# Gate and up products of the three FFNs as seven block products

## The chip, the core and the metric

The kernel runs on one core of a Trainium2 chip. Its time is the device time of one execution in microseconds (us), from the first to the last instruction. Every number of the kernel before comes from its three timed executions or from one execution that the hardware profiler recorded.

## What is computed

The reference is two transformer blocks in float32 on one sequence of 512 tokens with 1024 features. Each block has a mixer (two kinds of attention in the first, sparse attention and retention in the second); between and behind them lie three gated feed-forward networks (FFN), here called f0, f1 and f2, with 2816 hidden features:

```python
def swiglu(xn, w_gate, w_up, w_down):
    return (jax.nn.silu(xn @ w_gate) * (xn @ w_up)) @ w_down
...
h = rms_norm(x, g);  x = x + 1.0 * swiglu(h, ...)     # f0
h = _rmsnorm(x, g);  x = x + 0.5 * _swiglu(h, ...)    # f1 and f2
```

The two products `xn @ w_gate` and `xn @ w_up` (512 x 1024 by 1024 x 2816 each) are what the change touches.

## The kernel before

Features lie on the partitions: `xh[m]`, `xl[m]` (m = 0..7) are [128, 512] tiles that hold the normalised input (for the FFNs: gain times x, still without its rms) in two exact parts, high and low, and a weight tile is split in the same way. Every product is three matmuls, high x high, high x low and low x high (`mm3`, lines 241 to 245).

`Stream` (lines 141 to 189) brings in the weights in the order of their use, which `plan` (lines 330 to 415) lists. For each item SP issues one DMA into a `raw` tile (line 160, three buffers), ScalarE rounds it to the high part `wh` (line 172), VectorE subtracts for the low part `wl` (line 174, two halves), both in four buffers. `run_ahead` keeps the split two items ahead of the use.

`ffn` (lines 1022 to 1069) goes over two halves of 11 column blocks of 128 hidden features. For one block the gate and the up weights (128 columns, all 1024 rows, 512 KB each, 512-byte rows) are two items; each meets the eight input tiles in 8 x 3 matmuls of 512 columns, so a block is 48 matmuls. Then VectorE multiplies both sums by the rms (`rb`, lines 1042 and 1044), ScalarE takes a tanh (1043), GpSimd multiplies (1045), VectorE multiplies (1046), and the hidden block is split into `hh`, `hl` (1047 to 1052). After 11 blocks the down product runs over eight output tiles with 33 matmuls each (1056 to 1069); in f2's second half `last` (line 1636) does that with tokens on partitions. There are 3 x 22 = 66 such blocks.

In f1 the hook `each` (line 1593) also multiplies one residual tile in blocks 1 to 8. In f2 `out2` (line 1624) transposes the residual while the first half's down product runs. `rb` of an FFN is ready only in its second block (hooks `sums`, `spread`).

The order of instructions on each engine is made at build time by a list scheduler from the program's order and its dependences; every engine then works through its queue in order. The GpSimd queue (POOL) issues few DMAs: the residual's loads in `out_product` (line 1011) and some in the mixers.

Of the kernel before, what the change touches and what calls it, by code (L numbers as in the profile page):

```python
# [49 lines left out]
# columns of the constants  # L50
# [15 lines left out]
# the packed vectors, in pieces of 128  # L66
# [60 lines left out]

def _arrays(inputs):
    """The inputs as the chip takes them: x with features first, the small vectors side by side."""
# [6 lines left out]
    out["pos"] = np.ascontiguousarray(raw["positions"].reshape(NT, P).T)  # L136
    out["cst"], out["ret"], out["rot"] = _constants()
# [3 lines left out]
class Stream:  # L141
    """Weights in the order of their use: loads run ahead, and the split into two exact parts too."""

    def __init__(self, b, plan, raw_bufs, bufs, ahead):
        self.b, self.plan = b, plan
        self.raw_bufs, self.bufs, self.ahead = raw_bufs, bufs, ahead
        self.loaded = self.split = self.used = 0
        self.raw, self.parts = {}, {}

    def load_to(self, n):  # L150
        while self.loaded < min(n, len(self.plan)):
            i = self.loaded
            key, nk, nc_, srcs = self.plan[i]
            t = self.b.wpool.tile([P, 1024], F32, tag="raw", name=f"raw{i}", bufs=self.raw_bufs)
            v = t[:, :nk * nc_].rearrange("p (k n) -> p k n", k=nk)
            for (k0, k1, c0, c1, src) in srcs:
                dst = v[:, k0:k1, c0:c1]
                if key in ("qn", "qr", "kv"):
                    dst = v[:, k0, c0:c1].rearrange("p (h d) -> p h d", h=8)
                self.b.nc.sync.dma_start(out=dst, in_=src)  # L160
            self.raw[i] = (t, nk * nc_)
            self.loaded += 1

    def split_to(self, n):
        nc = self.b.nc
        while self.split < min(n, len(self.plan)):
            i = self.split
            self.load_to(i + 1)
            t, n_el = self.raw.pop(i)
            h = self.b.wpool.tile([P, 1024], F32R, tag="wh", name=f"wh{i}", bufs=self.bufs)  # L170
            lo = self.b.wpool.tile([P, 1024], F32R, tag="wl", name=f"wl{i}", bufs=self.bufs)
# [5 lines left out]
            self.load_to(self.split + self.raw_bufs)  # L177

    def next(self, key):
        i = self.used  # L180
        got, nk, nc_, _ = self.plan[i]
# [3 lines left out]
        h, lo = self.parts.pop(i)  # L185
        return tuple(a[:, :nk * nc_].rearrange("p (k n) -> p k n", k=nk) for a in (h, lo))

    def run_ahead(self):
        self.split_to(self.used + self.ahead)


class Build:
# [28 lines left out]
    def weave(self, main, fill, main_ns, fill_ns, k=1.0):  # L221
        """Interleave two generators of pieces by their share of TensorE's time."""
# [25 lines left out]
    def tgroup(self, acc, pairs, per=1):  # L248
        """pairs: (weight hi, weight lo, x hi, x lo) for each contraction tile"""
# [1461 lines left out]
```

## Time and profile before

| | |
|---|---|
| timed executions | 2122.47, 2123.30, 2123.37 us; median 2123.3 us |
| profiled execution | span 2124.0 us from first to last instruction, 0.7 us above that median |
| TensorE (PE) busy | 2084.2 us, 98% |
| VectorE (DVE) busy | 1359.0 us, 64% |
| ScalarE (ACT) busy | 895.5 us, 42% |
| GpSimd (POOL) busy | 395.1 us, 19% |
| mean transfer rate | 105 GB/s |

PE's busy time counts overlapping matmuls once; a matmul's own duration is longer than the distance to the next, so its pace is read from the starts of neighbours in the timeline. "PEclk" is the granted TensorE clock as a share of 2.4 GHz, "DMA share" the mean busy share of the 16 DMA engines.

### The profile page before, as it was taken

The numbers are of one execution on the slowest core, as the hardware profiler recorded it, in microseconds if no ns is written. First come the engines' busy times: TensorE is split into PE (matmuls) and PEld (weight loads), VectorE is DVE, ScalarE is ACT, GpSimd is POOL, SyncE is SP. The second block draws the span as 40 slices with busy tenths as digits, with TensorE's granted clock in tenths as the row PEclk, the third lists the DMA queues.
The fourth block names the chain that finished last, engine by engine and source line by source line (L and its number), as shares of the span: only waits on it lengthen the run. The fifth ranks groups of instructions, "written<-read, shape, count | busy, mean of one in ns | idle before, by whom it ended". The sixth has DMA issues, their size and how long they took to land.

```text
span 2124.0 us, 27104 instructions
## 1 busy us (share of the span) xinstructions
PE 2084.2 (98%) x9858; PEld 1716.7 (81%) x9858; DVE 1359.0 (64%) x2675; ACT 895.5 (42%) x1637; POOL 395.1 (19%) x360
## 2 busy tenths in 40 slices
PE   8999999999999999999998999999999999999998
PEld 7787878888888888888887778888888888888887
DVE  7778876654455565445547799888557765544655
ACT  5666753322222433223234476666343332323334
POOL 3233332110011220000115121110312221000110
PEclk9999999999999999999999999999999999999999
DMA  5323354332332333233245413222533443323344
GB/s 151 98 62 89 93 170 129 91 91 82 115 91 80 110 98 93 82 113 100 80 143 154 105 55 90 70 80 70 180 114 108 135 149 89 87 83 110 97 118 150
DMA packets 347782, 223.35 MB, mean 105 GB/s; under 512 B 16784, under 2 KB 326160, under 8 KB 347648
## 3 DMA queue, kind: packets, MB, share of 16 engines
q1 hardware_dynamic: 341264, 203.94, 33.4%
q0 software_dynamic: 5024, 15.90, 2.4%
q10 hardware_dynamic: 1360, 1.77, 0.3%
q8 instruction: 78, 1.28, 0.3%
q14 instruction: 56, 0.46, 0.1%
HBM read 204.11 MB, written 14.68 MB: 103 GB/s over the span
## 4 chain that ended last, share of the span: by engine, by line
PE 90%; DVE 4%; ACT 2%; issue 1%; DMA 1%; POOL 1%; SPq 0%; ACTq 0%; POOLq 0%; DVEq 0%
PE mm L243 25%; PE mm L245 25%; PE mm L244 24%; PE pt L477 2%; PE pv L496 1%; PE pv L497 1%; PE mm L1653 1%; PE s L1424 1%; PE s L1425 1%; PE pt L1653 1%; PE pv L1495 1%; DVE wl L174 1%; DMA raw<-in_w_in 1%; PE pt L538 0%; ACT P L459 0%
## 5 line engine op out<-in xcount | busy, mean ns | idle before, releaser
L243 PE MATMUL mm<-xh,wh 128*128 128x512 f32 x1752 | 704.7, 402 | 6.5 <-ACT kvg L1087 6.5
L174 DVE TENSOR_TENSOR wl<-raw,wh 128x512 fp32r<-128x512 f32 (+5 forms) x738 | 551.5, 777 | 216.6 <-ACT wh L172 215.6
L245 PE MATMUL mm<-xh,wl 128*128 128x512 f32 x1752 | 688.7, 393 | 0.0
L244 PE MATMUL mm<-xl,wh 128*128 128x512 f32 x1752 | 687.7, 393 | 0.0
L172 ACT CAST wh<-raw 128x1024 fp32r<-128x1024 f32 (+5 forms) x369 | 360.6, 977 | 734.7 <-PE mm L244 642.5
L245 PEld LDWEIGHTS mm<-xh,wl 128*128 128x128 f32 x1752 | 329.8, 188 | 73.4
L243 PEld LDWEIGHTS mm<-xh,wh 128*128 128x128 f32 x1752 | 330.8, 189 | 66.9 <-ACT kvg L1087 6.7
L244 PEld LDWEIGHTS mm<-xl,wh 128*128 128x128 f32 x1752 | 330.8, 189 | 59.9 <-DVE xl L217 0.6
L1045 POOL TENSOR_TENSOR fu<-fu,fg 128x512 f32<-128x512 f32 x66 | 88.5, 1341 | 809.5 <-DVE fu L1044 809.5
L1044 DVE TENSOR_TENSOR fu<-mm,rb 128x512 f32<-128x512 f32 x66 | 45.6, 691 | 208.5 <-PE mm L245 208.5
L243 PE MATMUL mm<-hh,wh 128*128 128x512 f32 x440 | 173.0, 393 | 0.0
L244 PE MATMUL mm<-hl,wh 128*128 128x512 f32 x440 | 172.2, 391 | 0.0
L245 PE MATMUL mm<-hh,wl 128*128 128x512 f32 x440 | 171.6, 390 | 0.0
L459 ACT ACTIVATE P<-s,st 128x128 f32<-128x128 f32 (+1 forms) x192 | 101.4, 529 | 63.7 <-DVE st L454 59.4
L212 ACT ACTIVATE hh<-ft 128x512 fp32r<-128x512 f32 x66 | 41.8, 633 | 167.0 <-DVE ft L1046 167.0
L210 ACT CAST ph<-pt 128x128 fp32r<-128x128 f32 x192 | 80.3, 425 | 51.3 <-PE pt L477 50.3
L217 DVE TENSOR_TENSOR pl<-pt,ph 128x128 fp32r<-128x128 f32 x192 | 91.6, 484 | 14.1 <-ACT ph L210 12.6
L454 DVE CUSTOM_DVE_ANT_0 s<-s,cst 128x128 f32<-128x128 f32 (+1 forms) x192 | 93.5, 490 | 8.8 <-PE s L1425 4.6
L245 PEld LDWEIGHTS mm<-hh,wl 128*128 128x128 f32 x440 | 82.6, 188 | 18.8
L243 PEld LDWEIGHTS mm<-hh,wh 128*128 128x128 f32 x440 | 82.7, 188 | 17.8
L244 PEld LDWEIGHTS mm<-hl,wh 128*128 128x128 f32 x440 | 82.7, 188 | 17.4
L477 PE MATMUL pt<-cst,P 128*128 128x128 f32 x480 | 83.4, 274 | 1.2 <-DVE pl L217 0.5
(415 smaller groups left out, 2843.0 us busy)
## 6 DMA issues: line engine op xcount, KB each, us to landing
raw<-in_w_in SPq DMA_DIRECT2D x79, 512.0 KB
raw<-in_ffn_w_gate SPq DMA_DIRECT2D x44, 512.0 KB
raw<-in_ffn_w_up SPq DMA_DIRECT2D x44, 512.0 KB
raw<-in_w_ffn_gate SPq DMA_DIRECT2D x22, 512.0 KB
raw<-in_w_ffn_up SPq DMA_DIRECT2D x22, 512.0 KB
raw<-in_ffn_w_down SPq DMA_DIRECT2D x22, 512.0 KB
raw<-in_ffn_w_down SPq DMA_DIRECT2D x24, 384.0 KB
sp_th<-gt SPq DMA_DIRECT2D x32, 256.0 KB
```

Source lines behind the costliest of these rows:

```text
L172: nc.scalar.copy(h[:, :n_el], t[:, :n_el])
L174: nc.vector.tensor_tensor(out=lo[:, a:e], in0=t[:, a:e], in1=h[:, a:e].bitcast(F32), op=ALU.subtract)
L210: self.nc.scalar.copy(out, in_)
L217: (eng or nc.vector).tensor_tensor(out=out, in0=in_, in1=hi.bitcast(F32), op=ALU.subtract)
L243: mm(acc, lhsT=lh, rhs=rh, start=start, stop=False)
L244: mm(acc, lhsT=lh, rhs=rl, start=False, stop=False)
L245: mm(acc, lhsT=ll, rhs=rh, start=False, stop=stop)
L454: nc.vector.tensor_tensor_reduce(out=b, in0=b, in1=u["mask"][:, 512 - n:512], scale=-u["scale"], scalar=3.0e38, op0=ALU.add, op1=ALU.min, ...
L459: nc.scalar.activation(p, b, AF.Exp, bias=st[:, 0:1], scale=-1.0, accum_out=st[:, 1:2])
L477: nc.tensor.transpose(b[:, j * P:(j + 1) * P], u[f"P{i}"][:, j * P:(j + 1) * P], self.ident)
L1044: nc.vector.tensor_tensor(out=u, in0=acc[1], in1=self.rb, op=ALU.mult)
L1045: nc.gpsimd.tensor_tensor(out=u, in0=u, in1=g, op=ALU.mult)
```

## The change

For 18 of the 22 column blocks of each FFN (all but the first four) the gate and up products together become one unit of seven block products (Winograd's form of Strassen's algorithm). The 2 x 2 matrix of weight blocks has gate and up as one index and the two halves of the 1024 input features as the other; the 2 x 2 matrix of input blocks has the halves of the features and the halves of the 512 tokens. One block product ("quarter") is 4 x 3 = 12 matmuls with 256 columns, so a unit is 84 matmuls.

The host lays out gate and up of a column block side by side, four pieces of [128, 512] a block: u (first and second half of features) and g (the same). From these the stream loads three tiles of 512 KB (X, A, Y) and one of 256 KB (D), in 4 KB and 2 KB rows, and forms the four weight sums in X and Y by four DMAs of 256 KB that add to their destination, issued on the GpSimd queue: two with a piece from memory, two from tile to tile (X on itself, X on Y). D has a buffer ring of its own. Raw buffers go from three to four.

The input sums T1 to T4 (`th`, `tl`, also in two parts) are made by `prepare_t`, one feature pair behind each of the four plain blocks; `prepare_b` then overwrites `xh`, `xl` with the input times the rms, eight tiles, when the four plain blocks are through. In a unit ScalarE copies three intermediate sums out of PSUM, and the D quarter of a unit is put behind the first two quarters of the next (`pending`, `flush`). GpSimd's multiplication per block falls away in units.

Smaller edits: the low part is subtracted in one instruction instead of two halves; f1's residual products go two at a time to blocks 6 to 9; f2's transposes move into `last`; comments are removed.

```diff
-RAW_BUFS, PART_BUFS, AHEAD = 3, 4, 2
+RAW_BUFS, PART_BUFS, AHEAD = 4, 4, 2
+NPLAIN = 4
...
+def _gated(g, u):
+    t = lambda w: w.reshape(2, 4, P, FF // P, P).transpose(3, 2, 0, 1, 4).reshape(FF // P, P, 2, 512)
+    return np.ascontiguousarray(np.concatenate([t(u), t(g)], 2))
...
+    AT = {"X": (512, 1024), "A": (1024, 1024), "Y": (1024, 1024), "D": (512, 512)}
...
+                at, n_el = self.AT[kind]
+                nc.sync.dma_start(out=t[:, :n_el], in_=self.plan[i][2].rearrange("p q n -> p (q n)")[:, at:at + n_el])
...
+    def sum_up(self):
+        add = lambda out, in_: self.b.nc.gpsimd.dma_start(out=out, in_=in_, accum_op=ALU.add)
+        while self.summed < self.loaded:
+            i = self.summed
+            kind = self.plan[i][1]
+            if kind in ("X", "Y"):
+                t = self.raw[i][0]
+                add(t[:, 0:512], self.plan[i][2][:, 0, :])
+                if kind == "X":
+                    self.x = t
+                add(t[:, 512:1024], t[:, 0:512] if kind == "X" else self.x[:, 512:1024])
+            self.summed += 1
...
-            for a, e in ((0, n_el // 2), (n_el // 2, n_el)):
-                nc.vector.tensor_tensor(out=lo[:, a:e], in0=t[:, a:e], in1=h[:, a:e].bitcast(F32), op=ALU.subtract)
+            nc.vector.tensor_tensor(out=lo[:, :n_el], in0=t[:, :n_el], in1=h[:, :n_el].bitcast(F32), op=ALU.subtract)
...
+    def quarter(self, acc, i, at, op, start):
+        wh, wl = self.ws.parts[i]
+        for k in range(4):
+            sl = slice(at + k * P, at + (k + 1) * P)
+            xh, xl = self.operand(op, k)
+            for n, (l, r) in enumerate(((wh, xh), (wh, xl), (wl, xh))):
+                self.nc.tensor.matmul(acc, lhsT=l[:, sl], rhs=r, start=start and k + n == 0, stop=k == 3 and n == 2,
+                                      skip_group_check=True)
+
+    def prepare_t(self, k, gain):
+        nc, V, G = self.nc, self.nc.vector, self.nc.gpsimd
+        y = self.small.tile([P, 2, 512], F32, tag="diag", name=self.nm("y"), bufs=1)
+        for j in range(2):
+            V.scalar_tensor_tensor(out=y[:, j, :], in0=self.xs[k + 4 * j], scalar=gain(k + 4 * j), in1=self.rb, op0=ALU.mult, op1=ALU.mult)
...
+        G.tensor_tensor(out=t[0][:, 0, :], in0=b11, in1=b12, op=ALU.subtract)
+        V.tensor_tensor(out=t[1][:, 0, :], in0=b22, in1=b12, op=ALU.subtract)
+        V.scalar_tensor_tensor(out=t[0][:, 1, :], in0=t[1][:, 0, :], scalar=-1.0, in1=b11, op0=ALU.mult, op1=ALU.subtract)
+        V.scalar_tensor_tensor(out=t[1][:, 1, :], in0=t[0][:, 1, :], scalar=-1.0, in1=b21, op0=ALU.mult, op1=ALU.subtract)
+        for j in range(2):
+            h = self.th[k][:, 2 * j:2 * j + 2, :]
+            self.hi(h, t[j])
+            self.lo(self.tl[k][:, 2 * j:2 * j + 2, :], t[j], h)
+
+    def prepare_b(self, gain):
+        for m in range(KD):
+            if m % 2 == 0:
+                y2 = self.small.tile([P, 2, 512], F32, tag="diag", name=self.nm("y"), bufs=1)
+            n = 256 if m < 4 else 512
+            y = y2[:, m % 2, 0:n]
+            self.nc.vector.scalar_tensor_tensor(out=y, in0=self.xs[m][:, 0:n], scalar=gain(m), in1=self.rb[:, 0:n], op0=ALU.mult, op1=ALU.mult)
+            self.hi(self.xh[m][:, 0:n], y)
+            self.lo(self.xl[m][:, 0:n], y, self.xh[m][:, 0:n])
+
+    def unit(self, key, hh, hl, i):
...
+        self.quarter(r1, A, 0, "B11", True)
+        nc.scalar.copy(e[:, 0:256], r1)
+        self.quarter(r23[:, 256:512], X, 0, "T1", True)
+        nc.scalar.copy(f, r23[:, 256:512])
+        self.flush()
...
+        self.quarter(r1, X, 512, "T2", False)
+        nc.scalar.copy(e[:, 256:512], r1)
...
+        self.quarter(r23[:, 0:256], A, 512, "B21", False)
...
+        self.quarter(r23[:, 256:512], Y, 512, "B22", False)
...
+        V.tensor_tensor(out=g, in0=r23, in1=e, op=ALU.add)
+        nc.scalar.activation(th, g, AF.Tanh, scale=0.5)
...
+        self.quarter(r1, Y, 0, "T3", False)
+        V.scalar_tensor_tensor(out=th, in0=th, scalar=1.0, in1=g, op0=ALU.add, op1=ALU.mult)
+        V.tensor_tensor(out=u2, in0=r1, in1=f, op=ALU.add)
+        V.tensor_tensor(out=th[:, 256:512], in0=th[:, 256:512], in1=u2, op=ALU.mult)
...
+        def rest():
+            self.quarter(r1, DD, 0, "T4", False)
+            V.tensor_tensor(out=th[:, 0:256], in0=th[:, 0:256], in1=r1, op=ALU.mult)
+            self.put_hidden(i, th, -0.5, hh, hl)
+            ws.release(DD)
+        self.pending = rest
...
-    nc = bacc.Bacc("TRN2", target_bir_lowering=False, num_devices=1)
+    nc = bacc.Bacc("TRN2", target_bir_lowering=False, num_devices=1, dynamic_dma_scratch_size=8192)
```

## Rows read from the trace of the kernel before

**Rows 1.** Page, part 1: busy us, share of span, instructions.
```profile
PE 2084.2 (98%) x9858; PEld 1716.7 (81%) x9858; DVE 1359.0 (64%) x2675; ACT 895.5 (42%) x1637; POOL 395.1 (19%) x360
```
**Rows 2.** Page, part 4: the chain that ended last, share by engine.
```profile
PE 90%; DVE 4%; ACT 2%; issue 1%; DMA 1%; POOL 1%; SPq 0%; ACTq 0%; POOLq 0%; DVEq 0%
```
**Rows 3.** Busy time by stretch, one column block of f0 each; last columns clock, DMA.
```profile
421.50:432.50 11.00, 11.00 (x49) 9.02 (x48) 6.41 (x9) 3.29 (x4) 1.30 (x1) 1.00 0.33 95
432.50:443.50 11.00, 11.00 (x49) 9.01 (x48) 6.41 (x9) 3.29 (x4) 1.30 (x1) 1.00 0.34 98
```
**Rows 4.** Timeline of ACT in f0: start, us, instruction, idle before it.
```profile
417.14 1.05 ACT L172 CAST wh<-raw 128x1024 fp32r<-128x1024 f32 x1 [3.85 <-PE mm L244]
...
428.13 1.05 ACT L172 CAST wh<-raw 128x1024 fp32r<-128x1024 f32 x1 [3.85 <-PE mm L244]
```
**Rows 5.** Timeline of PE in the last product: 256 columns between 512.
```profile
2086.76 0.28 PE L1653 MATMUL s<-wh,hh 128*128 128x256 f32 x1
...
2087.46 0.39 PE L1653 MATMUL pt<-wh,hh 128*128 128x512 f32 x1
...
2089.55 0.28 PE L1653 MATMUL s<-wh,hh 128*128 128x256 f32 x1
...
2090.26 0.39 PE L1653 MATMUL pt<-wh,hh 128*128 128x512 f32 x1
```
**Rows 6.** Groups by line and shape: count, busy us, mean ns, idle before.
```profile
L172 ACT CAST wh<-raw 128x1024 fp32r<-128x1024 f32 x275 | 289.2, 1052 | 527.7 <-PE mm L244 446.9 <-issue 38.4 <-PE pv L1653 14.0
...
L219 DVE SCALAR_TENSOR_TENSOR hl<-ft,hh 128x512 fp32r<-128x512 f32 x66 | 45.7, 692 | 13.5 <-ACT hh L212 8.4
...
L1043 ACT ACTIVATE ft<-fg 128x512 f32<-128x512 f32 x66 | 41.8, 633 | 4.9 <-DVE fg L1042 3.5
...
L217 DVE TENSOR_TENSOR pl<-pt,ph 128x256 fp32r<-128x256 f32 x48 | 19.8, 413 | 1.0 <-ACT ph L210 0.8
...
L210 ACT CAST ph<-pt 128x256 fp32r<-128x256 f32 x48 | 17.8, 372 | 9.6 <-PE pt L477 9.3
```
**Rows 7.** Timeline of DVE in f0: two weight subtractions, one beside GpSimd.
```profile
429.22 1.82 DVE L174 TENSOR_TENSOR wl<-raw,wh 128x512 fp32r<-128x512 f32 x1 [0.16 <-ACT wh L172]
...
434.76 1.29 DVE L174 TENSOR_TENSOR wl<-raw,wh 128x512 fp32r<-128x512 f32 x2 [0.21 <-ACT wh L172]
```
**Rows 8.** Busy time by stretch where DMA is fullest; last columns share, GB/s.
```profile
8.00:12.00 4.00, 2.84 (x17) 2.16 (x16) 3.44 (x5) 3.41 (x7) 3.34 (x3) 1.00 1.04 385
...
290.00:300.00 10.00, 8.88 (x39) 6.95 (x37) 7.25 (x12) 4.68 (x9) 2.75 (x6) 1.00 1.01 327
...
1120.00:1127.00 7.00, 7.00 (x50) 6.74 (x49) 3.97 (x7) 3.63 (x4) 3.71 (x4) 1.00 1.00 304
```
**Rows 9.** DMA issues on the GpSimd queue: count, KB, median us to landing.
```profile
thb<-sp_th POOLq DMA_DIRECT2D x16, 256.0 KB, 3.4
...
xs<-in_xT POOLq DMA_DIRECT2D x8, 256.0 KB, 6.1
```
**Rows 10.** One line's instructions, ns min/median/max: a GpSimd DMA's issue.
```profile
L1011 POOL DMA_DIRECT2D xs<-in_xT x8: 536/536/536, 288.1 to 291.9; - x8
```
**Rows 11.** Timeline of PE where the second mixer renormalises eight tiles.
```profile
1127.03 0.30 PE L432 MATMUL pv<-wh,xl 128*128 128x304 f32 x1
1133.79 0.79 PE L243 MATMUL mm<-xh,wh 128*128 128x512 f32 x1 [6.45 <-ACT kvg L1087]
1134.38 0.63 PE L244 MATMUL mm<-xl,wh 128*128 128x512 f32 x1
...
1138.57 0.39 PE L244 MATMUL mm<-xl,wh 128*128 128x512 f32 x1
```
**Rows 12.** Timeline of DVE in the same stretch: first and last of L319.
```profile
1125.78 6.61 DVE L319 SCALAR_TENSOR_TENSOR xs<-xs,gains,rb 128x512 f32<-128x512 f32 x3 [2.38 <-ACT rb L289]
...
1139.17 1.23 DVE L319 SCALAR_TENSOR_TENSOR xs<-xs,gains,rb 128x512 f32<-128x512 f32 x1
```
**Rows 13.** Busy time by stretch: behind that idle time; last columns clock, DMA.
```profile
1133.00:1140.00 7.00, 6.21 (x18) 4.96 (x19) 7.00 (x11) 6.96 (x16) 1.13 (x2) 0.61 0.25 76
```

More of the change, by code (lines that the diff above doesn't have):

```diff
@@ L141 @@
 class Stream:
+    AT = {"X": (512, 1024), "A": (1024, 1024), "Y": (1024, 1024), "D": (512, 512)}
     def __init__(self, b, plan, raw_bufs, bufs, ahead):
-        self.b, self.plan = b, plan
-        self.raw_bufs, self.bufs, self.ahead = raw_bufs, bufs, ahead
-        self.loaded = self.split = self.used = 0
+        self.b, self.plan, self.ahead = b, [], ahead
+        for item in plan:
+            if item[1] == "unit":
+                self.plan += [(f"{item[0]}{c}", c, item[2]) for c in "XAYD"]
+            else:
+                self.plan.append(item)
+        self.raw_bufs, self.bufs = {"": raw_bufs, "d": 2}, {"": bufs, "d": 1}
+        self.ring, self.place, self.of = [], [], {"": [], "d": []}
+        for i, item in enumerate(self.plan):
+            r = "d" if item[1] == "D" else ""
+            self.ring.append(r)
+            self.place.append(len(self.of[r]))
+            self.of[r].append(i)
+        self.loaded = self.split = self.used = self.summed = 0
+        self.was_split, self.free, self.done = {"": 0, "d": 0}, {"": 0, "d": 0}, set()
@@ L148, in __init__, with tile @@
         self.raw, self.parts = {}, {}
+    def tile(self, tag, i, bufs, dt):
+        r = self.ring[i]
+        pool = self.b.att if r else self.b.wpool
+        return pool.tile([P, 512 if r else 1024], dt, tag=tag + r, name=f"{tag}{r}{i}", bufs=bufs[r])
     def load_to(self, n):
+        nc = self.b.nc
         while self.loaded < min(n, len(self.plan)):
             i = self.loaded
-            key, nk, nc_, srcs = self.plan[i]
-            t = self.b.wpool.tile([P, 1024], F32, tag="raw", name=f"raw{i}", bufs=self.raw_bufs)
@@ L155, in load_to @@
[L155 to L161, printed above, removed]
-            self.loaded += 1
+            r = self.ring[i]
+            if self.place[i] >= self.was_split[r] + self.raw_bufs[r] or (r and self.b.att is None):
+                return
@@ new lines, in load_to @@
+            t = self.tile("raw", i, self.raw_bufs, F32)
+            kind = self.plan[i][1]
+            if isinstance(kind, str):
+                at, n_el = self.AT[kind]
+                nc.sync.dma_start(out=t[:, :n_el], in_=self.plan[i][2].rearrange("p q n -> p (q n)")[:, at:at + n_el])
+            else:
+                key, nk, nc_, srcs = self.plan[i]
+                n_el = nk * nc_
+                v = t[:, :n_el].rearrange("p (k n) -> p k n", k=nk)
+                for (k0, k1, c0, c1, src) in srcs:
+                    dst = v[:, k0:k1, c0:c1]
+                    if key in ("qn", "qr", "kv"):
+                        dst = v[:, k0, c0:c1].rearrange("p (h d) -> p h d", h=8)
+                    nc.sync.dma_start(out=dst, in_=src)
@@ L1019, in out_product, with operand @@
             self.sq_add(accs, xs[m], m == 0)
-    def ffn(self, tag, scale, hooks, on_out, each=None, last=None):
+    OPS = {"B11": 0, "B21": 1, "B22": 2, "T1": 3, "T2": 4, "T3": 5, "T4": 6}
+    def operand(self, op, k):
+        if op[0] == "T":
+            j = int(op[1]) - 1
+            return self.th[k][:, j, :], self.tl[k][:, j, :]
+        m = k + 4 * (op[1] == "2")
+        sl = slice(256 * (op[2] == "2"), 256 * (op[2] == "2") + 256)
+        return self.xh[m][:, sl], self.xl[m][:, sl]
@@ new lines, with flush, put_hidden, ffn @@
+    pending = None
+    def flush(self):
+        if self.pending is not None:
+            f, self.pending = self.pending, None
+            f()
+    def put_hidden(self, i, t, scale, hh, hl):
+        h = self.att.tile([P, 512], F32R, tag=f"hh{i}", name=self.nm("hh"))
+        l = self.att.tile([P, 512], F32R, tag=f"hl{i}", name=self.nm("hl"))
+        self.hi(h, t, scale=scale)
+        self.lo(l, t, h, scale=scale)
+        hh.append(h)
+        hl.append(l)
+    def ffn(self, tag, scale, gain, hooks, on_out, each=None, last=None):
@@ L1027, in ffn @@
             for i in range(11):
+                if half or i >= NPLAIN:
+                    self.unit(f"{tag}{half}{i}", hh, hl, i)
+                    if each is not None:
+                        each(half, i)
+                    continue
                 acc = []
@@ L1067, in ffn @@
                     nc.vector.scalar_tensor_tensor(out=x, in0=b, scalar=scale, in1=x, op0=ALU.mult, op1=ALU.add)
-                if half == 1 or last is not None:
+                if half == 1:
                     on_out(m, x)
@@ L1664, in last @@
                             products(w, k, q, n)
+                    if t == 0 and k == 0:
+                        self.flush()
+                        nc.gpsimd.dma_start(out=gb, in_=I["final_norm_2"][None, :].to_broadcast([P, D]))
+                    if t == 0:
+                        next(turned, None)
                 for q in range(4):
```

141 lines of the change are left out of this document (102 added, 39 removed).

## The prediction, made before the change was run

> **What bounds the kernel now.** I read the page's busy times first: PE is busy 98% of the span, no other engine over 64% [rows 1]. A busy PE need not be the bound, so the chain of waits comes next: 90% of the work that ended last is PE's [rows 2]. Then the stage that the change touches, cut into stretches of one column block: PE busy all of 11.00 us at full clock, DVE 6.41, ACT 3.29, POOL 1.30, the DMA engines a third full at 95 to 98 GB/s [rows 3]. The same ACT cast returns after 10.99 us [rows 4]; a block is 48 matmuls, so each costs 10.99 / 48 = 0.229 us and nothing else is waited for. In this stage PE time is time, and the three FFNs' 66 blocks take 725 us of the 2124.
>
> **PE in the units.** 54 blocks of 48 matmuls with 512 columns become 54 units of 84 with 256. Each matmul still loads its own weights (as many loads as matmuls [rows 1]), so half the columns need not cost half the time. Where the kernel already runs six matmuls of 256 columns in a row, they take 2087.46 - 2086.76 = 0.70 us and 2090.26 - 2089.55 = 0.71 us [rows 5]: 0.117 to 0.118 us each, full rate within 3%. A unit then takes 84 x 0.1175 = 9.87 us; I put 9.9 for a few hand-overs. The order of the quarters lets every PSUM copy finish under one or two other quarters (1.4 us each against 0.37 us a copy [rows 6]), so none is on the path. Saved: 54 x (10.99 - 9.9) = 58.9 us; bounds 60.5 (9.87) and, if waits of 0.3 us come in, 43.
>
> **ACT and DVE in a unit.** ACT: three casts of 1.05, one of half size and a tanh at 0.63, the hidden split 0.63, three PSUM copies 0.37 [rows 6]: 6.2 us. DVE: three subtractions of 1024 columns, at most 1.29 each [rows 7], one of 512, and three more 512-wide operations at 0.69 and three 256-wide at 0.41 [rows 6]: 3.9 + 2.8 + 1.2 = 7.9 us. Both lie under PE's 9.9; f1's residual products (about 1.5 us in four units) still fit. GpSimd's multiplication, beside which a subtraction took 1.82 us [rows 7], is gone from units. So the casts, sums and tanh are costed at nothing; their cover is PE's 9.9 us. The single subtraction, the fourth raw buffer, the moved transposes (as many as before) and the smaller descriptor space I cost at nothing too, within 3 us either way.
>
> **DMA in a unit.** Loads: 3 x 524 + 262 KB = 1.84 MB; sums: 4 x 262 KB = 1.05 MB; together 2.88 MB where a block moved 1.05. That no row shows an adding DMA is the largest gap here. Full engines moved 385, 327 and 304 GB/s [rows 8]. If an add costs what a copy of its bytes costs, a unit needs 7.5, 8.8 or 9.5 us of the DMA engines: under 9.9, though barely. If the old value has to be fetched through the same engines, the adds count twice, 3.93 MB, and a unit needs 10.2, 12.0 or 12.9 us: the DMA engines are then the bound. I take the copy's price, because the loads turn from 512-byte rows to rows of 2 and 4 KB and the 327 GB/s stretch is nearest to that; both ends stay in the range.
>
> The Trainium skill (Collectives: The Full Stack, section Part 3: Why 7x under link rate) speaks against me: a reducing DMA reads two sources, pushes two read descriptors a chunk through one ring, and comes out at about half a copy's rate. No run here shows it yet. By that rule the second set of times holds, and the change loses; it is the first rival below.
>
> **GpSimd's queue.** It holds nothing else in a unit, but each sum waits: the tile's load, its first add, its second. Issuing costs 0.54 us [rows 10]. A DMA of 256 KB on this queue landed after 3.4 us, with eight in a row after 6.1 [rows 9]. In order, two adds that are waited for and two that are only issued give 2 x 3.4 + 2 x 0.54 = 7.9 us a unit; at 4.4 us a landing it equals PE's 9.9, at 6.1 it is 13.3. Who waits behind: the cast of X or Y on ACT, and behind that the PSUM copies. I take 3.4 to 4.4, because each add has at most one other beside it.
>
> **The hand-over from plain blocks to units, once per FFN.** prepare_b overwrites the operands that the fourth plain block still reads, so its splits start when that block ends, and the third and fourth feature halves are needed by the fifth and sixth quarter. DVE's work from there: the block's own three operations, 2.1 us; four tiles of 256 columns, 4 x 2 x 0.41 = 3.3; four of 512, 4 x 2 x 0.69 = 5.5 [rows 6]. Before that prepare_t wants two multiplications, three 256-wide sums and two subtractions, 4.1 us a time, and one GpSimd sum that can hold DVE up; four of them are 17 us or more, while a plain block leaves 11.0 - 6.4 = 4.6 us of DVE [rows 3], and the rms comes only in the second block: 14 us of room. So some 3 to 4 us are left over. Together some 14.5 us, in which PE can do the four quarters that need no split of the later features, 5.6 us. PE stands some 9 us. The kernel has such a place: eight tiles renormalised from 1125.78 to 1140.40 [rows 12], PE idle 6.45 us, then eleven matmuls from 1133.79 to 1138.57 in 4.78 us instead of 2.52 [rows 11], mean granted clock 0.61 [rows 13], that is partly at 1.2 GHz. That adds 2.3 us. I take 11 us a time, 33 in all; the ends are 2 (the scheduler finds other work) and 17 (nothing overlaps), 6 and 51.
>
> **Sum.** 2124.0 - 58.9 + 33 = 2098.1 us in the profiled execution, 2097.4 on the median's scale: 2098.
>
> **The rivals.** First, slower: an add costs its bytes twice, the DMA engines set the pace. At 327 GB/s a unit takes 12.0 us: 2124 + 54 x (12.0 - 10.99) + 33 = 2212; at 304, 2260; at 385, 10.2 us and 2114. It decides from the rate at which a unit takes 10.99 - 33/54 = 10.38 us: 3.93 MB / 10.38 us = 379 GB/s. For it: an add must know the old value. Against: 385 was reached once, and reads and writes may overlap. Where DMA is nearly enough, units of 11.2 us give 2168. Second, the serial sums: landings of 4.7 us under the heavier traffic give 2 x 4.7 + 1.1 = 10.5 us a unit, 2124 - 26 + 33 = 2131: little or nothing is left. For it: 6.1 us under load [rows 9]; against: four raw buffers let the sums of two tiles overlap. Third, better: PE finds work at the hand-over, 2124 - 59 + 6 = 2071. For it: the scheduler moves independent work forward; against: DVE's backlog is real work.
>
> **How the numbers follow.** Forecast (2080 to 2115) 0.42; no stall at the hand-over (2062 to 2080) 0.16; serial sums (2115 to 2145) 0.16; DMA-bound (2145 and more) 0.26. Eight in ten: from 2068, which leaves out little, to 2172, which takes in the milder DMA-bound half. Runs of this kernel tell 0.2% from no change, 4.2 us: faster below 2119. The first two and a little of the third, 0.62; same 0.08; slower 0.30.
>
> **What would show it.** Right: starts of neighbouring 256-column matmuls in units 0.117 us apart; one unit per 9.9 us; an idle PE of 5 to 12 us with a lower clock behind it three times, in front of the fifth block of each FFN; the DMA share in units 0.75 to 0.95; adds landing within 4.4 us. Wrong: PE idle in every unit with ACT's casts waiting for an adding DMA, and a DMA share near 1.0 (first rival) or well under it (second); or DVE over 9 us in a unit, which would say that I mis-sized its work.

## The result, and the profile after

The changed kernel takes 2324.8 us (median of four runs, 2319.7 to 2326.5) against 2122.9 us: the ratio is 1.094 (95% interval 1.093 to 1.096). I had forecast 2098 and a range that ended at 2172.

Page of the kernel after: busy times, the chain by engine and by line, the GpSimd DMA queue (packets, MB, share of 16 engines), the adding DMAs (count, KB, median us from issue to landing):

```profile
PE 2113.2 (91%) x11802; PEld 1837.1 (79%) x11802; DVE 1448.5 (62%) x2654; ACT 1045.0 (45%) x1955; POOL 541.9 (23%) x534
...
q0 software_dynamic: 36128, 72.54, 16.9%
...
PE 58%; DMA 16%; DVE 11%; issue 7%; ACT 4%; POOL 2%; SPq 0%; ACTq 0%; POOLq 0%; DVEq 0%
...
raw<-in_gu_f POOLq DMA_DIRECT2D x108, 256.0 KB, 4.8
raw<-raw POOLq DMA_DIRECT2D x108, 256.0 KB, 5.5
```

Where the chain was 90% PE [rows 2], it is 58% now, and 16% of it are DMAs, which were 1%. PE is busy 29 us longer than before [rows 1] although it has less to do, and idle for 211 us.

Longest waits of the kernel after (us in total, times, longest):

```profile
POOL raw L213 <- DMA raw<-in_gu_f: 597.5, 94, 60.9
...
ACT wh L238 <- DMA raw<-raw: 312.7, 51, 10.1
...
PE mm L1134 <- ACT fu L1179: 133.2, 40, 7.0
```

Read from the bottom: PE waits for a PSUM copy on ACT; that copy stands on ACT behind a weight cast; the cast waits for the second sum; and GpSimd's queue waits for loads and first sums to land (the first row has both, since both write `raw` from `in_gu_f`). Eight units in the middle of f0's second half, from tanh to tanh, in a table of stretches as [rows 3] (length, then PE, PEld, DVE, ACT, POOL busy, clock, DMA share, GB/s):

```profile
613.97:731.50 117.53, 92.64 (x672) 90.97 (x672) 58.64 (x80) 44.71 (x74) 27.86 (x33) 0.85 0.82 196
```

A unit takes 117.53 / 8 = 14.69 us, where a block took 11.00 [rows 3] and I had put 9.9. PE is idle for 24.9 us of these, 3.1 a unit, and its 672 matmuls take 92.6 us in place of the 76.6 that they take when fed (first experiment): 2.0 us a unit at a granted clock of 0.85. One such place, timeline of PE (start, duration, operation, idle before it):

```profile
660.53 0.58 PE L1134 MATMUL mm<-th,wh 128*128 128x256 f32 x1 [5.49 <-ACT fu L1179]
660.91 0.42 PE L1134 MATMUL mm<-tl,wh 128*128 128x256 f32 x1
661.13 0.42 PE L1134 MATMUL mm<-th,wl 128*128 128x256 f32 x1
...
664.32 0.28 PE L1134 MATMUL pt<-xh,wl 128*128 128x256 f32 x1
664.43 0.28 PE L1134 MATMUL pt<-xh,wh 128*128 128x256 f32 x1
```

The two stretches (columns as above):

```profile
660.53:664.32 3.79, 3.79 (x18) 3.79 (x18) 3.07 (x6) 2.40 (x5) 0.00 (x0) 0.50 0.87 143
664.32:667.00 2.68, 2.68 (x24) 2.68 (x24) 1.92 (x2) 1.34 (x3) 0.87 (x1) 1.00 0.85 274
```

Behind 5.49 us of idle time the starts are 0.21 us apart at a granted clock of 0.50, 1.2 GHz; from 664.32 on they are 0.11 to 0.12 us apart at 1.00, 2.4 GHz. An idle PE is paid for twice.

The GpSimd queue over the same unit, and the loads that SP issued in it:

```profile
643.54 0.87 POOL L213 DMA_DIRECT2D raw<-in_gu_f  x1 [7.15 <-DMA raw<-in_gu_f]
644.08 1.23 POOL L213 DMA_DIRECT2D raw<-raw  x1
644.73 1.47 POOL L213 DMA_DIRECT2D raw<-in_gu_f  x1
650.72 0.86 POOL L213 DMA_DIRECT2D raw<-raw  x1 [4.53 <-DMA raw<-in_gu_f]
656.66 0.86 POOL L213 DMA_DIRECT2D raw<-in_gu_f  x1 [5.08 <-DMA raw<-in_gu_f]
658.75 0.86 POOL L213 DMA_DIRECT2D raw<-raw  x1 [1.23 <-DMA raw<-raw]
659.34 1.17 POOL L213 DMA_DIRECT2D raw<-in_gu_f  x1
...
649.22 0.33 SPq L198 DMA_DIRECT2D raw<-in_gu_f  x1
649.64 0.38 SPq L198 DMA_DIRECT2D rawd<-in_gu_f  x1
650.11 1.86 SPq L198 DMA_DIRECT2D raw<-in_gu_f  x2
```

In order the sums are Y's two of the unit before (643.54, 644.08), X's first sum (644.73), X's second (650.72), Y's first (656.66), Y's second (658.75) and the next X's first (659.34). X's second sum waits for the first to land, 6.0 us; Y's second waits for X's second, 8.0 us, because it reads it; the next unit's first sum stands behind both: 6.0 + 8.0 + 0.6 = 14.6 us, the unit. A second loop runs through the raw buffers. Y's second sum reads X's buffer, so the load into that buffer, that of the next unit's A, waits until it has landed (the Y sum issued at 644.08, the load at 649.22), and on SP's queue the load of the next Y stands behind that one (650.11, the first of two). Y's first sum (656.66) waits 5.08 us for that load, so this loop ends only 1.2 us before the other, the wait that is left in front of Y's second sum. One unit later it ends last, and Y's second sum goes out without a wait:

```profile
671.80 0.86 POOL L213 DMA_DIRECT2D raw<-in_gu_f  x1 [5.08 <-DMA raw<-in_gu_f]
672.80 0.87 POOL L213 DMA_DIRECT2D raw<-raw  x1
```

Over the kernel, SP's queue waits longest, for tiles of units, for second sums (us in total, times, longest):

```profile
SPq L198 <- DMA raw<-raw: 440.3, 67, 12.2
```

The experiments have to say which loop, and whether the adding DMAs are too dear or only too late.

### The profile page after: what moved, and what is told of

Read it like the earlier page. It is cut to its first block, busy times and chain, and to the rows that moved or that the text cites. A ratio compares the mean times of both kernels' runs of the same rounds, so it can differ in the third digit from the quotient of the medians.

```text
span 2324.3 us, 32124 instructions
## 1 busy us (share of the span) xinstructions
PE 2113.2 (91%) x11802; PEld 1837.1 (79%) x11802; DVE 1448.5 (62%) x2654; ACT 1045.0 (45%) x1955; POOL 541.9 (23%) x534
## 3 DMA queue, kind: packets, MB, share of 16 engines
q0 software_dynamic: 36128, 72.54, 16.9%
## 4 chain that ended last, share of the span: by engine, by line
PE 58%; DMA 16%; DVE 11%; issue 7%; ACT 4%; POOL 2%; SPq 0%; ACTq 0%; POOLq 0%; DVEq 0%
PE mm L331 12%; PE mm L332 12%; PE mm L333 12%; DMA raw<-raw 9%; DMA raw<-in_gu_f 7%; PE mm L1134 6%; DVE wl L239 3%; PE pt L1134 3%; ACT wh L238 2%; PE pt L569 2%; PE mm L1868 1%; PE pv L588 1%; PE pv L589 1%; POOL raw L213 1%; PE s L1635 1%
## 5 line engine op out<-in xcount | busy, mean ns | idle before, releaser
L239 DVE TENSOR_TENSOR wl<-raw,wh 128x1024 fp32r<-128x1024 f32 (+5 forms) x423 | 517.2, 1224 | 548.4 <-ACT wh L238 545.9
L331 PE MATMUL mm<-xh,wh 128*128 128x512 f32 x888 | 364.1, 410 | 6.2 <-ACT kvg L1298 6.2
L333 PE MATMUL mm<-xh,wl 128*128 128x512 f32 x888 | 351.8, 396 | 0.0
L332 PE MATMUL mm<-xl,wh 128*128 128x512 f32 x888 | 350.3, 395 | 0.0
L1134 PE MATMUL mm<-th,wh 128*128 128x256 f32 x432 | 141.5, 328 | 139.2 <-ACT fu L1179 133.2
L333 PEld LDWEIGHTS mm<-xh,wl 128*128 128x128 f32 x888 | 167.6, 189 | 36.0
L331 PEld LDWEIGHTS mm<-xh,wh 128*128 128x128 f32 x888 | 168.5, 190 | 32.6 <-ACT kvg L1298 6.5
L332 PEld LDWEIGHTS mm<-xl,wh 128*128 128x128 f32 x888 | 168.6, 190 | 25.2
L1134 PE MATMUL pt<-xh,wh 128*128 128x256 f32 x432 | 136.7, 316 | 10.1 <-ACT ff L1181 10.1
L1134 PE MATMUL mm<-th,wl 128*128 128x256 f32 x432 | 135.9, 315 | 0.0
L1134 PEld LDWEIGHTS pt<-xh,wh 128*128 128x128 f32 x432 | 98.9, 229 | 10.6 <-ACT ff L1181 10.5
```

The lines of the kernel that those rows point to most:

```text
L239: nc.vector.tensor_tensor(out=lo[:, :n_el], in0=t[:, :n_el], in1=h[:, :n_el].bitcast(F32), op=ALU.subtract)
L331: mm(acc, lhsT=lh, rhs=rh, start=start, stop=False)
L332: mm(acc, lhsT=lh, rhs=rl, start=False, stop=False)
L333: mm(acc, lhsT=ll, rhs=rh, start=False, stop=stop)
L1134: self.nc.tensor.matmul(acc, lhsT=l[:, sl], rhs=r, start=start and k + n == 0, stop=k == 3 and n == 2, skip_group_check=True)
```

## The experiments

Theories: A, the engines: an add costs its bytes twice, the DMA engines set the pace. B, the ring: a raw buffer takes load, first sum, second sum and cast in turn, and four are too few. C, the GpSimd queue: sums wait there for sums, in order. D, ACT's order: a cast that waits holds up PSUM copies. Shorthand in what follows: "unit" is the time from tanh to tanh in f0's second half.

**No sums.**

```diff
-            if kind in ("X", "Y"):
+            if False and kind in ("X", "Y"):
```

> Left out: the four weight sums of every unit (X and Y are used as loaded). Nothing else is changed, so this is the unit without any adding DMA. If all of the loss lies in the sums, by any mechanism, units run at PE's pace (84 x 0.1135 = 9.5 to 9.9 us, tanh to tanh) and the total is 2124 - 54 x (10.99 - 9.9) + 3 x 8 = 2089, at most 2098 with the 11 us of the prediction for a hand-over. If ACT's order (casts ahead of PSUM copies) or DVE's load costs time of itself, units stay over 10.4 us and the total is 2125 or more.

Measured: 2073.4 us (ratio 0.976, 0.974 to 0.977). Eight units:

```profile
578.09:654.68 76.59, 76.59 (x672) 76.59 (x672) 58.92 (x80) 46.32 (x74) 0.00 (x0) 1.00 0.59 188
```

A unit takes 9.57 us and PE is never idle. All of the loss, 2324.8 - 2073.4 = 251 us, lies in the four sums, and PE's, DVE's and ACT's terms were sound. It came out below my own expectation.

**The same DMAs without the addition.**

```diff
-... dma_start(out=out, in_=in_, accum_op=ALU.add)
+... dma_start(out=out, in_=in_)
```

> Left out: the addition in the four sums; the same four 256 KB DMAs on GpSimd's queue, same sources, same destinations, same waits, but they overwrite instead of adding. Doubled price of an add (theory A): the adds take 16.9% of the engines' span less 2.4% before, 342 us or 6.3 us a unit; as copies half, 3.2, so that a unit's DMA work falls from 11.8 (0.80 x 14.8) to 8.7 us and units become PE's: 2090 to 2120. Serial chain of load, first sum, second sum through four raw buffers (theory B): landings fall from 4.8 and 5.5 to the 3.4 that plain DMAs of this size and queue took before; a chain of some 17 us gets 3.5 us shorter, a unit 14.8 x 13.5 / 17 = 11.8 us: 2324 - 54 x 3 = 2160.

Measured: 2203.0 us (1.037, 1.035 to 1.039); units of 9.5 to 15.5 us. The queue's row without sums, then this run's page:

```profile
q0 software_dynamic: 5024, 15.90, 2.4%
...
q0 software_dynamic: 22304, 72.54, 10.1%
...
raw<-in_gu_f POOLq DMA_DIRECT2D x108, 256.0 KB, 3.7
raw<-raw POOLq DMA_DIRECT2D x108, 256.0 KB, 3.9
```

The price of an add is there. Without sums this queue took 2.4% of 2073 us, 50 us of all engines; so the sums take 16.9% of 2324 less 50, 343 us, in the kernel after, and 10.1% of 2199 less 50, 172 us, here: 6.4 and 3.2 us a unit. But without that price 130 of the 251 us remain. The waits carry at least half, with plain landings of 3.7 to 3.9 us.

**Seven raw buffers.** To make room there is one part buffer less, and D's raw tile and the tanh have one buffer.

```diff
-RAW_BUFS, PART_BUFS, AHEAD = 4, 4, 2
+RAW_BUFS, PART_BUFS, AHEAD = 7, 3, 2
-        self.raw_bufs, self.bufs = {"": raw_bufs, "d": 2}, {"": bufs, "d": 1}
+        self.raw_bufs, self.bufs = {"": raw_bufs, "d": 1}, {"": bufs, "d": 1}
...
-        g, th, u2 = tl("fg", 512), tl("ft", 512, 2), tl("fw", 256)
+        g, th, u2 = tl("fg", 512), tl("ft", 512), tl("fw", 256)
...
```

> Seven raw buffers in place of four, paid for with three part buffers in place of four and single buffers for the raw D tile and the tanh. The adds stay. Theory B (too few buffers for the latency of the chain): the ring is 7/4 as deep, a unit falls to what the engines or GpSimd's queue allow, 11.8 us (DMA share near 1.0) and the total to about 2160 to 2200. Theory C, GpSimd's queue in order (each second sum waits there for the first one's landing, 2 x 4.8 + 2 x 0.95 = 11.5 us and more): the same place, 12 to 13 us a unit and 2190 to 2230, with the share under 0.95. Theory A alone (engines are full when they work): no change, over 2290.

Measured: 2243.8 us (1.056, 1.054 to 1.058). Behind the first unit of the half come 9.7 and 12.5 us, as long as the reserve lasts, then 14.5 to 16.1 again. In this steady part GpSimd's queue has the same two waits as above:

```profile
647.69 0.87 POOL L213 DMA_DIRECT2D raw<-raw  x1 [4.22 <-DMA raw<-in_gu_f]
...
656.62 0.87 POOL L213 DMA_DIRECT2D raw<-raw  x1 [7.15 <-DMA raw<-raw]
```

Y's first sum no longer waits for a load here; the queue's chain sets the unit. The ring alone is not it.

**Second sums from memory.** Other sums, same bytes, none that reads a sum.

```diff
-                add(t[:, 512:1024], t[:, 0:512] if kind == "X" else self.x[:, 512:1024])
+                add(t[:, 512:1024], self.plan[i][2][:, 1, :])
```

> Changed: the second sum of X and of Y takes its addend from memory (another piece of the same block) in place of the tile that was summed first; so no second sum has to wait for a first one's landing. The sums are other sums; bytes, count and kind of the DMAs are the same, only 14 MB of tile-to-tile traffic become loads. Theory A: no change, 2290 to 2330. Theory B or C: X and Y are ready one landing (4.8 us) earlier, a unit takes 14.8 x 12 / 17 = 10.5 to 12 us: 2090 to 2170.

Measured: 2271.3 us (1.069, 1.067 to 1.071), most units 12.1 to 15.4 us. SP's waits for the tiles of units, and the landing of the adds:

```profile
SPq L198 <- DVE wl L239: 428.3, 151, 10.9
...
raw<-in_gu_f POOLq DMA_DIRECT2D x216, 256.0 KB, 7.6
```

The edit takes away more than the queue's chain: Y's second sum no longer reads X's buffer, so that buffer is free after its own split. What SP waits for now is that split, the weight subtraction (`wl`); and with sums that go out in close order a landing takes 7.6 us. With four buffers the round of load, sums, cast and subtraction alone still makes 14 us, so the queue's chain alone is not it either.

**Both edits together** (seven raw buffers, second sums from memory).

> Both earlier edits: seven raw buffers, and second sums from memory, so that GpSimd's queue never waits for one sum before the next and the ring is deep. What is left is the engines' own work. Changed: the sums are other sums, bytes and kinds as after. Theory A (engines): the adds cost 6.3 us and the loads 5.5 us of all 16 engines a unit, so a unit takes 11.8 to 12.5 us, the DMA share is 0.95 to 1.0 in units, and the total is 2073 + 54 x (2.2 to 2.9) = 2190 to 2230, above the kernel before: even without any wait the adds lose. Theory B (waits): units at 9.6 to 10 us, share under 0.9, total 2073 to 2100.

Measured: 2117.7 us (0.997, 0.996 to 0.999). Six units and the landing of its adds:

```profile
602.02:660.07 58.05, 58.05 (x504) 57.94 (x503) 43.56 (x60) 34.00 (x55) 21.15 (x24) 1.00 1.09 292
...
raw<-in_gu_f POOLq DMA_DIRECT2D x216, 256.0 KB, 8.9
```

A unit takes 9.68 us with the same number, kind and bytes of adding DMAs. The engines are full (1.09) and the adds land later than ever, 8.9 us, and PE does not stand for a moment. Theory A is refuted as the bound of this kernel: twice the price, but under PE. One edit saved 81 us, the other 53, both 207: there are two loops of nearly the same length, one through GpSimd's queue and one through the raw buffers, and each hides the other. The 44 us to the kernel without sums lie outside the units for the most part (f0's first tanh comes at 400.4 instead of 392.5 us, for one); the buffer counts differ too, and I haven't split that further.

**Copies with seven raw buffers** (the second and the third edit).

> Left out: the addition in the sums (plain DMAs as in the run of copies), here with seven raw buffers. Theory A with a chain on top: copies cost 3.2 us a unit beside 5.5 us of loads, 8.7 under 9.6, and the serial landings of 3.7 and 3.9 us with four issues of 0.9 make 2 x 3.8 + 2 x 0.9 = 9.4 us: units close to PE's 9.6, total 2073 to 2110. If the chain alone sets the unit (theory B or C), nothing changes against the copies with four buffers: 2190 to 2205.

Measured: 2125.0 us (1.001, 1.000 to 1.002). Units of 9.6 us until the reserve is used, then 10 to 11.7: 78 us less than with four buffers, and no better than dearer adds that do not wait for each other. Leaving out the addition saves 122 us with four buffers and 119 us with seven, as long as sums wait for sums. So the price of an add mattered through its landing (4.8 and 5.5 us against 3.7 and 3.9) in a chain that waits for landings.

**ACT's order.** Y's cast put behind the copies of the first two quarters:

```diff
-        ws.split_to(c + 3)
+        ws.split_to(c + 2)
...
-        ws.split_to(c + 7)
-        ws.go_on()
```

> The kernel after with one move: the cast of Y is put behind the copies of the first two quarters and no longer in front of the tanh's successors, so that ScalarE's queue doesn't hold PSUM copies behind a cast that waits for a sum. If that order is a cause of its own (PE stands 3.1 us a unit behind it and then runs at a lower clock), the unit loses up to 4 us: 2110 to 2200. If the rate is set by load, sum, sum in four buffers, PE only waits elsewhere: 2290 to 2330.

Measured: 2325.3 us (1.094, 1.092 to 1.097), no change. But ACT's order had hardly changed either. The same place in the kernel after and in this run:

```profile
658.64 1.04 ACT L238 CAST wh<-raw 128x1024 fp32r<-128x1024 f32 x1 [8.29 <-DMA raw<-raw]
659.60 0.62 ACT L1195 ACTIVATE ft<-fg 128x512 f32<-128x512 f32 x1
660.13 0.35 ACT L1179 COPY fu<-mm 128x256 f32<-128x256 f32 x1
...
658.42 1.04 ACT L238 CAST wh<-raw 128x1024 fp32r<-128x1024 f32 x1 [8.92 <-DMA raw<-raw]
659.37 0.62 ACT L1195 ACTIVATE ft<-fg 128x512 f32<-128x512 f32 x1
659.90 0.35 ACT L1179 COPY fu<-mm 128x256 f32<-128x256 f32 x1
```

The list scheduler put the cast back: over the whole kernel, ACT's instructions stand in the same order in both traces, by operation and tile, but for three in one place, and the casts that wait for second sums stand where they stood. This run tests nothing, and D stays open in part: without sums, in units of the same order on ACT, PE was never idle, so the order costs nothing as long as no cast is late; what it adds when casts are late was not tested.

**Another order on GpSimd's queue.** Seven raw buffers; the next tile's first sum in front of this tile's second one (`self.wait` keeps tiles whose second sum is due).

```diff
+                self.b.nc.gpsimd.dma_start(out=self.raw[i][0][:, 0:512], in_=self.plan[i][2][:, 0, :], accum_op=ALU.add)
+                self.second(i - 4)
+                self.wait.append(i)
```

> The whole computation, the same four adding DMAs a unit, seven raw buffers; only their order on GpSimd's queue differs: the first sum of the next unit's X (Y) is issued before the second sum of this unit's X (Y), so that a second sum finds the first one landed. One landing a unit is left in the queue (Y's second sum behind X's). If the chain is the cause, units go from 14.7 to 9.8 to 11 us and the total from 2244 to 2120 to 2180; if adds are slow as such, it stays within 30 us of 2244.

Measured: 2238.2 us (1.053, 1.050 to 1.055), nothing: the list scheduler had put the sums back into the old order, X's two and then Y's two, as the same two waits in front of second sums show, so this run tests nothing:

```profile
647.52 0.88 POOL L231 DMA_DIRECT2D raw<-raw  x1 [4.25 <-DMA raw<-in_gu_f]
...
656.31 0.87 POOL L231 DMA_DIRECT2D raw<-raw  x1 [7.01 <-DMA raw<-raw]
```

With the order held by edges (`with tc.issue_after(last add)` around each add):

> The whole computation, the same four adding DMAs a unit from the same sources, seven raw buffers; the order first sum of the next X (Y), second sum of this X (Y) is now held on GpSimd's queue by order edges. If the unit's 14.7 us are the two landings that are waited for in the queue, only one is left (Y's second sum behind X's): 9.8 to 11 us a unit, total 2120 to 2180 against 2244. If it is the rate of adding DMAs, it stays within 30 us of 2244.

Measured: 2258.5 us (1.063, 1.061 to 1.066); most units 12.3 to 15.3 us. GpSimd now waits once a unit:

```profile
651.48 0.88 POOL L228 DMA_DIRECT2D raw<-in_gu_f  x1 [10.90 <-DVE wl L258]
652.02 1.24 POOL L228 DMA_DIRECT2D raw<-raw  x1
652.55 1.60 POOL L228 DMA_DIRECT2D raw<-in_gu_f  x1
653.09 1.97 POOL L228 DMA_DIRECT2D raw<-raw  x1
...
665.24 0.88 POOL L228 DMA_DIRECT2D raw<-in_gu_f  x1 [10.18 <-DMA raw<-in_gu_f]
```

By my criterion this said "rate". The rows say otherwise: four adds go out within 2 us, and over the kernel first and second sums land after 5.0 and 5.7 us, hardly later than one by one. What is waited for is a load: with my order, Y's second sum stands behind the next Y's first, which needs the load of that Y, which stands on SP's queue behind a load into X's buffer, which waits for the Y sum before. I had closed another loop of about the same length. That the order of four tile-to-tile sums can be mended was therefore not shown.

**Second sums on VectorE.** The two first sums stay DMAs from memory; seven raw buffers.

```diff
-                add(t[:, 512:1024], t[:, 0:512] if kind == "X" else self.x[:, 512:1024])
...
+                nc.vector.tensor_tensor(out=t[:, 512:1024], in0=t[:, 512:1024],
+                                        in1=t[:, 0:512] if kind == "X" else self.x[:, 512:1024], op=ALU.add)
             nc.scalar.copy(h[:, :n_el], t[:, :n_el])
```

> The whole computation. First sums of X and Y stay adding DMAs from memory; the second sums are VectorE additions of 512 columns in front of the casts. Seven raw buffers, three part buffers. Two adds instead of four: engines 5.5 + 3.1 = 8.6 us a unit, under PE's 9.6; no sum waits for another on GpSimd's queue; VectorE 7.37 + 2 x 0.69 = 8.75 us. All theories then give units near 9.6 to 10.2 and a total of 2075 to 2110, under the kernel before. If a landing under load is too long for the ring, casts wait and the total is over 2125.

Measured: 2268.7 us (1.069, 1.067 to 1.070). I blamed the buffers, which were given back three at a time, and gave them back one by one, with both additions (X's, then Y's) in front of X's cast:

> The whole computation. First sums as adding DMAs from memory (two a unit, none waits for another), second sums both on VectorE in front of X's cast, and a raw buffer is given back after its own split, not after Y's. Seven raw buffers. VectorE 7.37 + 1.38 = 8.75 us under PE's 9.6. If the time of the earlier half-and-half run was its late loads (three buffers given back at once, so that Y had one unit of 9.6 us for a load and a sum of 5 us each), units fall to 9.6 to 10 us and the total to 2075 to 2100, under the kernel before. If two adds a unit are still too slow, casts wait and it stays over 2125.

Measured: 2265.7 us (1.066, 1.064 to 1.068); the buffers were not it. The timeline of DVE shows what was:

```profile
648.33 0.69 DVE L239 TENSOR_TENSOR raw<-raw 128x512 f32<-128x512 f32 x1 [4.25 <-DMA raw<-in_gu_f]
648.94 0.42 DVE L1203 TENSOR_TENSOR fw<-mm,ff 128x256 f32<-128x256 f32 x1
```

DVE stands at X's sum, and the unit's own `fw`, on which PE's next quarter depends, stands behind it. The scheduler had moved the X sums forward by about one unit: in the steady part each stands ahead of three casts and three or four weight subtractions that come before it in the program. Held in its place by an order edge (`self.last` is the last weight subtraction ahead of it):

```diff
+                with self.b.tc.issue_after(self.last.ins):
                     nc.vector.tensor_tensor(out=t[:, 512:1024], in0=t[:, 512:1024], in1=t[:, 0:512], op=ALU.add)
```

> The whole computation. Two adding DMAs a unit, from memory; both second sums on VectorE behind the last weight subtraction that stands ahead of them in the program, so that they can't be moved two units ahead. VectorE 8.75 us under PE's 9.6; engines about 8.6 us. If the earlier 2266 came from VectorE standing at a sum that was issued too early, units fall to 9.6 to 10.2 us and the total to 2075 to 2110, under the kernel before; if loads and sums are late as such, over 2150.

Measured: 2121.6 us (0.999, 0.998 to 1.000): 144 us from one edge. Eight units:

```profile
598.22:675.92 77.70, 77.70 (x675) 77.70 (x674) 67.46 (x96) 47.23 (x73) 11.34 (x13) 1.00 0.84 232
```

They take 9.71 us, as expected, but the total is 40 us over what such units should give (2073 + 54 x 0.14 = 2081): f0's first tanh comes at 405.4 us against 392.5 without sums, and f2's at 1770.1 against 1728.4. So the next runs changed the buffers (`RAW_BUFS, PART_BUFS` of 5, 4 and of 4, 4):

> The whole computation, as in the pinned half-and-half run, with five raw and four part buffers (D's raw tile and the tanh single). If three part buffers cost the mixers their 25 to 30 us, f0 starts near 392 us again and the total is 2080 to 2100, under the kernel before by 1 to 2%. If five raw buffers are too few for a load of 5 us and a sum of 5.7 us, units grow to 10.5 us and more and the total stays at 2120 or over.

> The whole computation with all buffers as in the kernel after (four raw, four part): only the two second sums are on VectorE, held in their place, in place of the two tile-to-tile DMAs. From a raw buffer's return to its next cast there are 4/3 of a unit, 12.8 us at 9.6 us a unit, against a load of 5 us, an issue of 0.9 and a landing of 5.7, 11.6 us: just enough, 9.7 to 10.5 us a unit and 2080 to 2125. If the chain needs a deeper ring, 11 to 12 us a unit and 2150 to 2200; about 2320 would say that the tile-to-tile sums were not the cause.

Measured: five raw and four part buffers 2119.9 us (0.998, 0.997 to 0.999), units 10 to 12 us; four and four 2161.5 us (1.018, 1.016 to 1.019), units 9.9 to 12.6 us, 11.4 in the mean, but f0's first tanh at 391.6. More raw buffers shorten the units, as B says, and cost something in front of them; what exactly they cost there, I did not find. The first of these is the best whole computation that I have: 205 us under the kernel after, 3.4 us under the kernel before, less than 0.2%.

**All sums on VectorE.** First out of their place, with raw buffers given back three at a time, then held in their place (six raw and three part buffers both times; the diff is the second run's):

```diff
+                    u0 = self.u0[i] = self.b.att.tile([P, 512], F32, tag="u0", name=f"u0{i}", bufs=2)
+                    nc.sync.dma_start(out=u0, in_=self.plan[i][2][:, 0, :])
...
+                    nc.vector.tensor_tensor(out=t[:, 0:512], in0=t[:, 0:512], in1=self.u0[i], op=ALU.add)
+                    nc.vector.tensor_tensor(out=y[:, 0:512], in0=y[:, 0:512], in1=self.u0[i], op=ALU.add)
```

> The whole computation. All four sums are VectorE additions of 512 columns; the piece u0 is loaded beside X (256 KB more), no adding DMA is left; six raw buffers, three part buffers. Engines about 6.3 us a unit; VectorE 7.37 + 4 x 0.69 = 10.1 us, over PE's 9.6: VectorE becomes the bound, units of 10.1 to 10.5 us, total 2073 + 54 x (0.5 to 0.9) = 2100 to 2122.

> The whole computation. No adding DMA: all four sums on VectorE at X's cast, in their place in the program, u0 loaded beside X. VectorE 7.37 + 4 x 0.69 = 10.1 us a unit is over PE's 9.6: units of 10.1 to 10.5 us, total 2073 + 54 x (0.5 to 0.9) = 2100 to 2122, a little under the kernel before; earlier it was 2151 with sums out of their place.

Measured: 2150.8 us (1.012, 1.010 to 1.014) and 2144.1 us (1.010, 1.008 to 1.011); pinned units of 10.33 us, in the expected band. Eight of them:

```profile
597.36:679.93 82.57, 79.89 (x672) 78.31 (x672) 75.98 (x113) 46.42 (x74) 0.00 (x0) 1.00 0.61 199
```

VectorE is busy for 9.5 us of a unit and PE for 10.0, so neither is full; that VectorE is the bound is not shown. The total is 22 us over the band. Part of it lies in front of f0 again (first tanh at 402.3 us, 10 later than without sums), part in the hand-overs, where the step from the fourth plain block's tanh to the first unit's is 6.6 to 7.5 us longer than without sums.

**Four raw and four part buffers, three and then four sums on VectorE** (the last diff without its last line and Y's first sum as a DMA again; the last diff whole).

> The whole computation. Four raw and four part buffers. X's two sums and Y's second one on VectorE, held in their place, one adding DMA a unit (Y's first sum); u0 is loaded beside X into a ring of two, D's raw tile and the tanh are single. VectorE 7.37 + 3 x 0.69 = 9.4 us, PE 9.6. If the latency of load plus adding DMA in four buffers made the 11.4 us of the half-and-half run with these buffers, X now needs 5 us in place of 11.6 and units fall to 9.7 to 10.3 us, total 2085 to 2115. If adds were not the cause, units stay at 11 us and the total at 2150 or over.

> The whole computation. As the pinned run with all sums on VectorE, with four raw and four part buffers in place of six and three. VectorE 7.37 + 4 x 0.69 = 10.1 us a unit sets the pace: 10.2 to 10.6 us as before (10.33), the mixers get their 10 us and more back that three part buffers cost: 2105 to 2130.

Measured: 2172.4 us (1.023, 1.022 to 1.025) and 2164.1 us (1.019, 1.017 to 1.020). Both miss. Most units take 11 to 13.5 us and 11.5 us, the latter without one adding DMA and at a DMA share of 0.60. So with four raw buffers something besides landings holds a unit at 11.5 us when sums lie on VectorE; DVE waits 1.7 us a unit for PE in it. That the half-and-half run with four buffers took 11.4 us because of landings is therefore not shown.

## Why the prediction was wrong, point by point

- **PE in the units: right, a little better.** 76.59 us / 672 = 0.114 us a matmul against 0.1175; 9.57 us a unit against 9.9.
- **ACT and DVE: right.** 46.3 / 8 = 5.8 and 58.9 / 8 = 7.4 us a unit against 6.2 and 7.9.
- **The hand-over: right in kind and size.** In the kernel after PE stands 5.90 us in front of the first unit of f0 (row below). Without sums, 2124.8 - 54 x (10.99 - 9.57) + 3h = 2073.4 gives h = 8.4 us, with whatever else changed once per FFN, against the 11 that I took (ends 2 and 17).
- **The price of an add: wrong, and it cost time through the landings, not through full engines.** I took a copy's price; measured, it is twice that, 6.4 us of the engines a unit against 3.2; leaving out the addition alone gave 122 of the 251 us back. The Trainium skill (Collectives: The Full Stack, Part 3: Why 7x under link rate) says of the reducing DMAs of a ring collective that they read two sources and come out at about half a copy's rate; the trace agrees in the price. The rival that I built on it, DMA-bound units, does not hold: the share in the kernel after was 0.82, and with the same adds at 1.09 units took 9.68 us.
- **GpSimd's queue: the step that failed.** I had the mechanism, two landings that are waited for and two that are only issued, and the point where it turns, 4.4 us a landing. I mis-sized the landing: 3.4 to 4.4 us, "because each add has at most one other beside it". In the unit shown, two adds of the unit before went out just ahead of X's first sum (643.54, 644.08), and beside X's second lay four tile loads (649.22 to 651.97), which the landings themselves release; how much each adds, no run separates. The two waits are 6.0 and 8.0 us; the rival with 4.7 us gave 10.5 us a unit, and it was 14.6. The issue was mis-sized too: 0.86 us for an adding DMA; the plain ones at the same line took the 0.54 that I had assumed.
- **The fourth raw buffer at nothing: wrong.** "Four raw buffers let the sums of two tiles overlap" was my argument against the serial sums. I had not followed a buffer around: X's is held until Y's second sum has landed, and SP's queue stands behind that. Second sums from memory end that hold together with the queue's chain, and four buffers still make 12 to 15 us a unit. What the hold costs by itself, no run shows.
- **What the queue's term lacked: the clock.** At the hand-over I had added 2.3 us for it; a stall in a unit I priced at its length. Here 3.1 us of idle time a unit bring 2.0 us of slower matmuls.

PE in front of the first unit of f0, kernel after:

```profile
430.84 0.58 PE L1134 MATMUL mm<-xh,wh 128*128 128x256 f32 x1 [5.90 <-ACT xh L298]
```

Of my signs, the wrong ones came true as written: PE idle in every unit, casts waiting for an adding DMA, a DMA share under 1.0 (its 0.82 also lies in the band that I had named for a right forecast, so it tells nothing apart). That pointed to the serial sums, and both edits together confirm that the waits, not the engines, set the pace. How much of the 251 us each loop would take alone cannot be said, since they overlap, and whether ACT's order adds to it was not tested.

## What to carry to other kernels

Follow a prefetched tile around its whole loop, from the return of its buffer to the next return, and count every transfer that another one waits for at its landing time under load, not its bytes at the engines' rate; a deeper ring alone gave back 81 of 251 us here, second sums that wait for no first one alone 53, and TensorE ran without a stall only when both loops were shorter than the work that they feed. When work is moved to an in-order engine, look in the trace where the scheduler has put it: one addition a unit that stood a unit too early cost 144 us here, and two runs measured an order that the scheduler had taken back. And price a stall of TensorE with the slower matmuls behind it.

## What the runs showed of the hardware

- A DMA of 256 KB that adds to its destination took 0.86 us to issue on GpSimd's queue, a plain one 0.54; its packets took twice the engines' time (6.4 and 3.2 us for four); it landed after 4.8 to 5.5 us where the plain one took 3.7 to 3.9.
- The landing of an add depends on what runs beside it: 5.0 and 5.7 us (medians over the kernel) in the run whose queue issued four within 2 us, 7.6 us with second sums from memory and four raw buffers, 8.9 us with seven. In the last, at a DMA share of 1.09, PE's units took 0.1 us more than without any add.
- Behind 5.49 us of idle time, TensorE's matmuls of 256 columns started 0.21 us apart at a granted clock of 0.50 and later 0.11 to 0.12 apart at 1.00; in eight units, 3.1 us of idle time a unit came with 2.0 us of slower matmuls.
